# One ring of seven buffers for weight and conditioning tiles, and a conditioning rate of 0.6 in the state-space stage

## The chip, the cores and the metric

The kernel runs on one core of one Trainium2 chip. The metric is device time in microseconds (us); lower is better. Three runs of the kernel before gave a median of 2463.67 us (2461.16 to 2466.41).

## The reference, cut to what matters

A trunk of two layers in float32 on 256 tokens of 2048 channels. Each layer has a token mixer and a squared-ReLU MLP. Each of these four sub-layers sees a normalised input that is shifted and scaled, and its output is added through a gate. The shifts, scales and gates come from a conditioning vector `c`, through a matrix of 2048 x 12288 for each layer.

```python
cond = jax.nn.silu(c)
for i in range(DEPTH):                       # 2 layers
    mod = cond @ ada_w[i] + ada_b[i]         # (2048) x (2048, 12288)
    sh1, sc1, g1, sh2, sc2, g2 = jnp.split(mod, 6, axis=-1)
    h = modulate(rmsnorm(x, ln1_g[i]), sh1, sc1)
    y = stick_breaking_mixer(...) if i == 0 else s5_mixer(...)
    x = x + g1[:, None, :] * y
    h = modulate(rmsnorm(x, ln2_g[i]), sh2, sc2)
    x = x + g2[:, None, :] * sq_relu_mlp(h, mlp_w1[i], mlp_w2[i])
```

Mixer 0 is stick-breaking attention (`sb_w_in` 2048 x 6144, `sb_w_out` 2048 x 2048). Mixer 1 is a diagonal state-space layer, called S5 (`s5_w_in` 2048 x 2048), then a gated linear unit, GLU (`s5_w_glu` 2048 x 4096). Each MLP has two matrices of 2048 x 8192 and 8192 x 2048.

## The kernel before, in words

**Weight tiles.** Every large product is cut into tiles of 512 KB (1024 float32 in each of 128 partitions). `weights` (L126) loads one into a buffer `w`, with a DMA issued on SyncE's queue (L129). ScalarE rounds it to `wh` (L131) and VectorE forms the rest `wl = w - wh` (L133). TensorE then runs 24 matmuls of 256 or 258 columns (`cols_tile`, L160 to L162), or 12 of 512 (`gemm_rows`, L146 to L148). A buffer `w` is free again when L133 has read it. There are `nw` = 3 buffers `w`, and `nh` = 3 each of `wh` and `wl`, which become free when TensorE has read them.

**Ticks and stages.** After each weight tile `tick` (L101) runs: one tick for one weight tile, 736 in all. In this order: attention 128 ticks (96 of `sb_w_in`, 32 of `sb_w_out`), the MLP of layer 0 with 256, the S5 stage with 32 (`s5_w_in`, beside the state-space work), the GLU with 64, and the MLP of layer 1 with 256.

**Conditioning tiles.** `ada_load` (L262) loads 512 KB of `ada_w` into a buffer `adaw`, of which there are 4 (apart from a pool of 8 that only the first 16 tiles use). There are 384 such tiles, 32 for each of twelve vectors (shift, scale and gate of four sub-layers). From the first MLP on a tile is read by one VectorE instruction, which multiplies it by the conditioning vector and adds it to an accumulator `adsums` or `adacc` (L356; L354 for a first one). In the attention stage it takes two instructions of half the size (L368, L370), or, for some tiles, TensorE reads it (L296). A generator for each vector (`ada_dve`, `ada_pe`) yields after each tile. `pump` (L396), called in each tick, adds `rate` to a credit and takes one tile from the queue of generators for each whole credit. `drain` takes all that a stage still needs, at once. Two units after a vector's last tile TensorE sums its accumulators over the partitions (`totals`, L323), and the accumulators are free again; there are three of them from the first MLP on, each serving 16 tiles.

**Rates.** Attention runs at 0.85 and later 1.3. The MLP of layer 0 begins at 1.0, and at 0.42 from its 17th tick on (`between`). The S5 stage runs at 0.35, the GLU at the number of tiles left over 44 ticks (`pace(44, mid[-1])`, L1122), and the MLP of layer 1 at what is left over 140 ticks (L1253).

**Order.** TensorE and GpSimd keep the order in which the program is written. The instructions of SyncE, VectorE and ScalarE are ordered when the program is built: at each step the planner gives an engine the earliest instruction in the program whose operands and buffers are at hand by its reckoning. A load has no operand to wait for, only a buffer. That order is then fixed; on the chip each queue runs it one after the other.

Of the kernel before, what the change touches and what calls it, by code (L numbers as in the profile page):

```python
# [8 lines left out]
F32 = mybir.dt.float32  # L9
# [7 lines left out]
P = 128  # L17
# [39 lines left out]
class Trunk:  # L57
# [203 lines left out]

    def ada_load(self, layer, vec, g, t, wide=False):  # L262
        start = g == 0 and vec < 2 and layer == 0
        wt = (self.ap0 if start else self.wp).tile([P, 2, 512], F32, name="adaw", bufs=8 if start else 4)
        c0 = vec * D + g * 512
        w = self.i["ada_w"][layer]
        if wide:
            self.nc.sync.dma_start(wt, w[t * P:t * P + P, c0:c0 + 1024].rearrange("p (a b) -> p a b", a=2))
        else:
            self.nc.sync.dma_start(wt, w[2 * t * P:2 * t * P + 2 * P, c0:c0 + 512].rearrange("(a p) b -> p a b", p=P))  # L270
        return wt
# [910 lines left out]

    def run(self):
        nc = self.nc
        self.nw, self.nh = 3, 3
        self.rate, self.credit, self.pending = 0.0, 0.0, {}
        self.recorder, self.early = None, True
        self.left, self.acts, self.unit, self.sums, self.turn = {}, [], 0, None, 0
        self.now, self.plan = 0, {}
        self.ctx.enter_context(self.tc.manual_schedule(engines={mybir.EngineType.PE, mybir.EngineType.Pool}))  # L1190
        st = ExitStack()
        self.ap0 = st.enter_context(self.tc.tile_pool(name="ap0", bufs=6))
        self.logexp()
        self.consts()
        self.xT = self.pers.tile([P, NB, S], F32, name="xT")
        self.mod = [self.pers.tile([P, 96], F32, name="mod%d" % l) for l in range(2)]
        sets = [self.ada(0, [(1, g), (0, g)], on_pe=bool(5 >> g & 1)) for g in range(4)]
        gates = [self.ada(0, [(4, g), (3, g), (4, g + 1), (3, g + 1)], on_pe=bool(0 >> (g // 2) & 1)) for g in (0, 2)]
        self.queue += sets + [self.ada_vec(0, 2, on_pe=bool(0))] + gates
        with self.tc.tile_pool(name="tmp0", bufs=1) as self.sp_:  # L1200
            self.condition()
            for _ in range(4):
                self.step(sets[0])
            x = self.load_x()
            self.vectors()
            for _ in range(6):
                self.step(sets[0])
            self.flip_x(x)
            self.rms_rows()
        self.drain(sets[0])  # L1210
        st.close()
        self.open_h(self.pers)
        self.modulate(0, 4)
        self.attention(sets, gates[0])
        self.dump("x1")
        M = lambda i: bool(0 >> i & 1)
        self.sums = self.ctx.enter_context(self.tc.tile_pool(name="sums", bufs=1))
        mid = [self.ada_vec(1, 4, M(4)), self.ada_vec(1, 3, M(5))]
        nxt = [self.ada_vec(1, 1, M(1)), self.ada_vec(1, 0, M(2))]
        self.queue += [self.ada_vec(0, 5, M(0))] + nxt + [self.ada_vec(1, 2, M(3))] + mid  # L1220
        last = self.ada_vec(1, 5, M(6))
        self.dram = self.ctx.enter_context(self.tc.tile_pool(name="dram", bufs=1, space=bass.MemoryType.DRAM))
        self.rate = 1.0

        stp = ExitStack()

        def params():
            tmp = stp.enter_context(self.tc.tile_pool(name="s5t", bufs=1))
            self.s5_tables(tmp)

        def between():
            self.drain(gates[1])
            self.shifts(8, 16, 0, 1)
            for kb in range(8, 16):
                self.fold(kb, 0, 1)
            self.rate = 0.42
            params()

        def ready():
            self.recorder.play(None)  # L1240
            stp.close()
            self.drain(*nxt)
            self.open_h(self.pers)
            self.shifts(0, 16, 1, 0)

        self.mlp(0, nxt=ready, between=between)
        self.dump("x2")
        self.rate = 0.35
        self.s5_mixer(mid)
        self.dump("x3")  # L1250
        self.logexp()
        self.queue.append(last)
        self.pace(140, last)  # L1253
        self.rows_open()
        self.mlp(1, last=True)
# [28 lines left out]
```

## Time and profile before

| what | value |
|---|---|
| median of 3 runs | 2463.67 us (2461.16 to 2466.41) |
| profiled execution | 2467.97 us, its span 2466.1 us |
| TensorE (PE) busy | 2365.1 us, 96% of the span |
| VectorE (DVE) busy | 1795.4 us, 73% |
| ScalarE (ACT) busy | 1212.7 us, 49% |
| GpSimd (POOL) busy | 316.6 us, 13% |
| granted TensorE clock | 0.989 of full speed, mean |
| moved by DMA | 627.09 MB, 254 GB/s on average |

The page is of one execution. The stages need different things, so its averages say little of any of them; the rows further down cut the span into stages. Matmuls overlap one another, so a TensorE that shows busy all the time is not at its peak; a gap in it is time lost for certain. "DMA" in a row is the mean busy share of the core's 16 DMA engines.

### The profile page before, as it was taken

The numbers are of one execution on the slowest core, as the hardware profiler recorded it, in microseconds if no ns is written. First come the engines' busy times: TensorE is split into PE (matmuls) and PEld (weight loads), VectorE is DVE, ScalarE is ACT, GpSimd is POOL, SyncE is SP. The second block draws the span as 40 slices with busy tenths as digits, with TensorE's granted clock in tenths as the row PEclk, the third lists the DMA queues.
The fourth block names the chain that finished last, engine by engine and source line by source line (L and its number), as shares of the span: only waits on it lengthen the run. The fifth ranks groups of instructions, "written<-read, shape, count | busy, mean of one in ns | idle before, by whom it ended". The sixth has DMA issues, their size and how long they took to land.

```text
span 2466.1 us, 45235 instructions
## 1 busy us (share of the span) xinstructions
PE 2365.1 (96%) x18355; PEld 2160.4 (88%) x18355; DVE 1795.4 (73%) x2223; ACT 1212.7 (49%) x1814; POOL 316.6 (13%) x340
## 2 busy tenths in 40 slices
PE   7999999999998999889999999989999999999999
PEld 4777789899988899889998998989998998998987
DVE  5789999999778767875786668888744554555554
ACT  4534875346334335435546776434554543543543
POOL 0000110001056545445300000000000000000000
PEclk9999999999999999999999999999999999999999
DMA  9888899999999967997798544999856555556565
GB/s 341 302 299 306 288 308 320 322 303 294 310 310 315 300 207 230 309 299 219 259 316 276 174 154 159 314 329 314 281 175 192 184 186 190 175 179 193 180 195 164
DMA packets 416773, 627.09 MB, mean 254 GB/s; under 512 B 19858, under 2 KB 282420, under 8 KB 414260
## 3 DMA queue, kind: packets, MB, share of 16 engines
q1 hardware_dynamic: 411968, 606.16, 74.8%
q0 software_dynamic: 3968, 17.83, 2.2%
q8 instruction: 144, 2.36, 0.4%
q14 instruction: 65, 0.53, 0.1%
q10 hardware_dynamic: 628, 0.21, 0.0%
HBM read 607.34 MB, written 16.78 MB: 253 GB/s over the span
## 4 chain that ended last, share of the span: by engine, by line
PE 44%; DMA 6%; DVE 5%; issue 3%; ACT 0%; SPq 0%; DVEq 0%; ACTq 0%
PE acc L160 9%; PE acc L162 8%; PE acc L161 8%; DMA adaw<-in_ada_w 5%; PE acc L146 5%; PE acc L148 5%; PE acc L147 5%; DVE wl L133 2%; PE mp L1053 1%; DVE adsums L356 1%; PE mp L1078 1%; PE mp L1038 1%; PE mp L1015 1%; DVE xT L435 1%; DMA w<-in_s_w_glu 0%
## 5 line engine op out<-in xcount | busy, mean ns | idle before, releaser
L131 ACT ACTIVATE wh<-w 128x1024 fp32r<-128x1024 f32 x736 | 777.5, 1058 | 1030.9 <-PE acc L162 364.6
L133 DVE TENSOR_TENSOR wl<-w,wh 128x1024 fp32r<-128x1024 f32 x736 | 922.6, 1255 | 436.9 <-ACT wh L131 434.3
L160 PE MATMUL acc<-hH,wl 128*128 128x258 f32 (+1 forms) x2816 | 808.4, 287 | 28.4 <-DVE wl L133 26.1
L162 PE MATMUL acc<-hH,wh 128*128 128x258 f32 (+1 forms) x2816 | 799.2, 284 | 0.0
L161 PE MATMUL acc<-hL,wh 128*128 128x258 f32 (+1 forms) x2816 | 797.8, 283 | 0.2 <-DVE hL L123 0.2
L160 PEld LDWEIGHTS acc<-hH,wl 128*128 128x128 f32 x2816 | 535.8, 190 | 44.3 <-DVE wl L133 33.6
L161 PEld LDWEIGHTS acc<-hL,wh 128*128 128x128 f32 x2816 | 536.3, 190 | 0.6 <-DVE hL L123 0.4
L162 PEld LDWEIGHTS acc<-hH,wh 128*128 128x128 f32 x2816 | 534.8, 190 | 0.0
L160 PE MATMUL acc<-aH,wl 128*128 128x256 f32 x1024 | 294.3, 287 | 26.4 <-DVE wl L133 25.5
L161 PE MATMUL acc<-aL,wh 128*128 128x256 f32 x1024 | 289.5, 283 | 0.0
L162 PE MATMUL acc<-aH,wh 128*128 128x256 f32 x1024 | 289.4, 283 | 0.0
L356 DVE SCALAR_TENSOR_TENSOR adsums<-adaw,cond,adsums 128x1024 f32<-128x1024 f32 x150 | 199.1, 1328 | 53.6 <-DMA adaw<-in_ada_w 53.0
L160 PEld LDWEIGHTS acc<-aH,wl 128*128 128x128 f32 x1024 | 194.3, 190 | 34.1 <-DVE wl L133 33.7
L146 PE MATMUL acc<-wh,aL 128*128 128x512 f32 x512 | 202.2, 395 | 0.0
L148 PE MATMUL acc<-wh,aH 128*128 128x512 f32 x512 | 202.1, 395 | 0.0
L147 PE MATMUL acc<-wl,aH 128*128 128x512 f32 x512 | 202.0, 395 | 0.0
L161 PEld LDWEIGHTS acc<-aL,wh 128*128 128x128 f32 x1024 | 194.4, 190 | 0.0
L162 PEld LDWEIGHTS acc<-aH,wh 128*128 128x128 f32 x1024 | 194.2, 190 | 0.0
L370 DVE SCALAR_TENSOR_TENSOR adacc<-adaw,cond,adacc 128x512 f32<-128x512 f32 x240 | 179.2, 750 | 3.1 <-DMA adaw<-in_ada_w 1.3
L146 PE MATMUL acc<-wh,hL 128*128 128x512 f32 x384 | 157.5, 410 | 5.8 <-ACT wh L131 3.1
L147 PE MATMUL acc<-wl,hH 128*128 128x512 f32 x384 | 153.8, 401 | 3.3 <-DVE wl L133 3.2
L148 PE MATMUL acc<-wh,hH 128*128 128x512 f32 x384 | 152.9, 398 | 0.0
(311 smaller groups left out, 2751.0 us busy)
## 6 DMA issues: line engine op xcount, KB each, us to landing
w<-in_mlp_w SPq DMA_DIRECT2D x512, 512.0 KB, 4.0
adaw<-in_ada_w SPq DMA_DIRECT2D x384, 512.0 KB, 6.0
w<-in_sb_w_in SPq DMA_DIRECT2D x96, 512.0 KB, 5.2
w<-in_s_w_glu SPq DMA_DIRECT2D x64, 512.0 KB, 5.4
w<-in_sb_w_out SPq DMA_DIRECT2D x32, 512.0 KB, 5.7
w<-in_s_w_in SPq DMA_DIRECT2D x32, 512.0 KB, 4.8
pw<-W POOLq DMA_DIRECT2D x8, 1024.0 KB, 6.5
W<-pw SPq DMA_DIRECT2D x8, 1024.0 KB, 7.7
```

The source lines that it names most:

```text
L131: nc.scalar.activation(h, w, AF.Copy)
L133: nc.vector.tensor_tensor(l, w, h.bitcast(F32), op=OP.subtract)
L146: nc.tensor.matmul(o, aL(kb)[:, s], H[:, kk], start=(kb == k0), stop=False)
L147: nc.tensor.matmul(o, aH(kb)[:, s], L[:, kk], start=False, stop=False)
L148: nc.tensor.matmul(o, aH(kb)[:, s], H[:, kk], start=False, stop=(kb == k1 - 1))
L160: nc.tensor.matmul(o, L[:, kk, s], aH(kb), start=(kb == k0), stop=False)
L161: nc.tensor.matmul(o, H[:, kk, s], aL(kb), start=False, stop=False)
L162: nc.tensor.matmul(o, H[:, kk, s], aH(kb), start=False, stop=(kb == k1 - 1))
L356: nc.vector.scalar_tensor_tensor(acc, wt, c, acc, op0=OP.mult, op1=OP.add)
L370: nc.vector.scalar_tensor_tensor(acc, wt[:, kk], c, acc, op0=OP.mult, op1=OP.add)
L435: nc.vector.scalar_tensor_tensor(x, y, self.mod[layer][:, vec * 16 + kb:vec * 16 + kb + 1], x, op0=OP.mult, op1=OP.add)
L1015: nc.tensor.transpose(pe[:, q * P:q * P + P], E[:, c, q].rearrange("p j a e -> p (j a e)"), self.ident)
```

## The change

The buffers of the two kinds of tile become one set. `nw` goes from 3 to 7, and `ada_load` takes its tile under the name `w`, with the same count, instead of `adaw` with 4. Both tiles have 4 KB in each partition, so the memory is the same (3 + 4 = 7). The first 16 tiles keep their own pool. The rate in the S5 stage goes from 0.35 to 0.6.

```diff
     def ada_load(self, layer, vec, g, t, wide=False):
         start = g == 0 and vec < 2 and layer == 0
-        wt = (self.ap0 if start else self.wp).tile([P, 2, 512], F32, name="adaw", bufs=8 if start else 4)
+        wt = self.ap0.tile([P, 2, 512], F32, name="adaw", bufs=8) if start else self.wp.tile([P, 2, 512], F32, name="w", bufs=self.nw)
...
     def run(self):
         nc = self.nc
-        self.nw, self.nh = 3, 3
+        self.nw, self.nh = 7, 3
...
         self.mlp(0, nxt=ready, between=between)
         self.dump("x2")
-        self.rate = 0.35
+        self.rate = 0.6
         self.s5_mixer(mid)
```

## Rows read from the trace of the kernel before

**Rows 1.** The page's 40 equal slices of the span, 61.65 us each.

```profile
PE   7999999999998999889999999989999999999999
...
DVE  5789999999778767875786668888744554555554
...
DMA  9888899999999967997798544999856555556565
GB/s 341 302 299 306 288 308 320 322 303 294 310 310 315 300 207 230 309 299 219 259 316 276 174 154 159 314 329 314 281 175 192 184 186 190 175 179 193 180 195 164
```

**Rows 2.** Windows by stage: length, busy time of each engine, clock, DMA share, GB/s.

```profile
0.00:491.10 491.10, 462.51 (x2441) 366.48 (x2442) 422.13 (x717) 266.69 (x524) 24.27 (x41) 0.98 0.92 311
491.10:592.00 100.90, 98.70 (x784) 94.50 (x783) 95.37 (x169) 53.82 (x79) 4.79 (x6) 1.00 0.92 305
592.00:1303.40 711.40, 672.04 (x5482) 659.34 (x5481) 552.77 (x559) 311.57 (x386) 282.45 (x282) 0.99 0.85 279
1303.40:1476.30 172.90, 167.02 (x2565) 154.97 (x2564) 114.07 (x153) 121.09 (x244) 5.13 (x11) 0.99 0.61 199
1476.30:1716.40 240.10, 225.58 (x2394) 215.63 (x2392) 201.65 (x247) 112.95 (x176) 0.00 (x0) 0.99 0.81 277
1716.40:1815.70 99.30, 94.89 (x774) 94.69 (x775) 71.19 (x75) 52.94 (x74) 0.00 (x0) 0.97 0.78 255
```

**Rows 3.** The same windows, conditioning tiles (adaw) alone: PE, PEld and DVE work.

```profile
592.00:1303.40 711.40, 0.00 (x0) 0.00 (x0) 164.65 (x121) 0.99 0.85 279
1303.40:1476.30 172.90, 0.00 (x0) 0.00 (x0) 3.85 (x3) 0.99 0.61 199
1476.30:1716.40 240.10, 0.00 (x0) 0.00 (x0) 78.50 (x63) 0.99 0.81 277
1716.40:1815.70 99.30, 0.00 (x0) 0.00 (x0) 21.25 (x17) 0.97 0.78 255
```

**Rows 4.** Windows of 16 ticks each, columns as in Rows 2.

```profile
1007.20:1061.50 54.30, 48.93 (x396) 47.10 (x394) 47.28 (x45) 19.79 (x23) 30.63 (x28) 1.00 0.91 311
...
1157.30:1204.20 46.90, 46.90 (x394) 46.90 (x393) 30.64 (x31) 25.67 (x34) 21.43 (x22) 1.00 0.67 211
...
1557.90:1611.00 53.10, 49.72 (x411) 48.06 (x409) 44.55 (x56) 22.11 (x30) 0.00 (x0) 1.00 0.97 332
...
1906.10:1952.20 46.10, 46.10 (x361) 44.92 (x361) 23.79 (x23) 23.75 (x29) 0.00 (x0) 1.00 0.60 185
```

**Rows 5.** Two of those windows, conditioning tiles alone.

```profile
1007.20:1061.50 54.30, 0.00 (x0) 0.00 (x0) 18.90 (x13) 1.00 0.91 311
...
1557.90:1611.00 53.10, 0.00 (x0) 0.00 (x0) 20.05 (x17) 1.00 0.97 332
```

**Rows 6.** Waits of SyncE's queue, 592 to 907 us: total us, times, longest.

```profile
SPq L129 <- DVE wl L133: 212.6, 95, 5.8
```

**Rows 7.** Waits of the engines, 592 to 907 us.

```profile
ACT wh L131 <- DMA w<-in_mlp_w: 106.0, 48, 5.6
```

**Rows 8.** DMA issues, 592 to 907 us, last column: median us from issue to landing.

```profile
w<-in_mlp_w SPq DMA_DIRECT2D x97, 512.0 KB, 5.0
adaw<-in_ada_w SPq DMA_DIRECT2D x61, 512.0 KB, 6.2
```

**Rows 9.** Groups of instructions on the page: busy us, mean ns, idle before.

```profile
L131 ACT ACTIVATE wh<-w 128x1024 fp32r<-128x1024 f32 x736 | 777.5, 1058 | 1030.9 <-PE acc L162 364.6
L133 DVE TENSOR_TENSOR wl<-w,wh 128x1024 fp32r<-128x1024 f32 x736 | 922.6, 1255 | 436.9 <-ACT wh L131 434.3
...
L356 DVE SCALAR_TENSOR_TENSOR adsums<-adaw,cond,adsums 128x1024 f32<-128x1024 f32 x150 | 199.1, 1328 | 53.6 <-DMA adaw<-in_ada_w 53.0
```

**Rows 10.** Chain of waits, 1040 to 1090 us: start, us, what.

```profile
1057.27 0.37 SPq L129
1057.68 10.39 DMA adaw<-in_ada_w
```

**Rows 11.** Waits of SyncE's queue, 185 to 491 us.

```profile
SPq L270 <- DVE adacc L370: 68.8, 64, 4.8
```

## The prediction

> **What bounds the kernel now.** I read the page's slices first (counted from 0). TensorE reads 8 tenths in slices 12, 16, 17 and 26; there the DMA engines read 9, and so they do in all of slices 5 to 13. In slices 14, 18, 19 and 22 to 24 it is the other way round: TensorE reads 9, and the DMA engines 4 to 7, with 154 to 259 GB/s [rows 1]. So the kernel swings between stretches that wait for data and stretches in which the DMA engines have time to spare. The windows by stage give the sizes [rows 2]. The second window (attention's end is at 491 us) and the first are VectorE's as much as the DMA's: 95.4 of 100.9 us busy there. From 592 to 1303 us, 224 ticks of the first MLP take 711.4 us, 3.18 us a tick. The GLU takes 240.1 us for 64 ticks. The S5 stage, 1303 to 1476 us, moves 199 GB/s and has TensorE nearly full.
>
> The third view is conditioning work by stage [rows 3]: 121 instructions in the 224 MLP ticks, 3 in the S5 stage, 63 in the GLU, 17 in the next 99 us. By the rates it should be otherwise: 224 x 0.42 = 94, and 32 x 0.35 = 11 in the S5 stage. Conditioning runs ahead of its pace. The reason lies in the order that the planner makes: a weight load waits for one of three buffers, a conditioning load finds one of its own four free, and so it goes first, until the three accumulators are full and TensorE's `totals` must empty one. So conditioning comes in bursts: 13 tiles in one 16-tick window [rows 5], none in another; the first takes 54.3 us, the second 46.9 [rows 4].
>
> The fourth view is the waits. Between 592 and 907 us SyncE's queue stands 212.6 us, in 95 waits, for a weight buffer that VectorE has not yet released [rows 6], and ScalarE waits 106.0 us for weights still on their way [rows 7]. A weight tile holds its buffer for 5.0 us of transfer [rows 8] and at least 1.06 + 1.26 us of rounding and subtraction [rows 9], 7.3 us, and longer where a wait lies between. Three buffers then give a tile each 2.4 us at the very best; with 2 us of waiting, each 3.1. The chain shows a wait at its worst: a conditioning load issued 0.4 us after a weight load takes 10.39 us to land [rows 10], and VectorE, in its fixed order, holds the next subtraction behind it.
>
> **The change part by part.** *One ring.* Both loads now ask for the same seven buffers and neither has anything else to wait for. So the earliest in the program gets the next one, and the loads go out in program order: conditioning keeps its pace. No instruction is added or removed; 384 and 736 loads stay. What moves is when. In program order 154 conditioning tiles are out when the first MLP begins, 16 more by its 17th tick at 1.0 and 7 by its 33rd at 0.42, 177 in all (180 today, from 384 - 121 - 3 - 63 - 17). The next 224 ticks bring 94 (today 121). I take the terms stage by stage.
>
> *224 ticks of the MLP.* The floor is the window without conditioning: 46.9 us for 16 ticks, 2.93 us a tick, TensorE without a gap, GpSimd's table work beside it [rows 4]. Can the DMA engines keep up? A window with weights alone has a share of 0.60 over 46.1 us, so a weight tile takes 27.7 / 16 = 1.73 us of the 16 engines. With 17 conditioning tiles beside 16 weights, 0.97 x 53.1 = 51.5 us; less the weights, 23.8 / 17 = 1.40 us for one of them [rows 4, 5]. The tables' transfers: 0.67 x 46.9 - 27.7 = 3.7 us in 16 ticks, 0.23 a tick [rows 4]. Sum: 1.73 + 0.42 x 1.40 + 0.23 = 2.55 us in a tick of 2.93, 87%. VectorE: 552.8 us of work today [rows 2] less 27 x 1.33 us, in some 660 us. So TensorE bounds this stretch, and a ring that holds about five weights (7 / 1.42) ahead covers a landing of 6 us and even one of 10. The bounds: 224 x 2.93 = 656 us, a gain of 55; or, if 87% of the engines is already too close to their end, the 3.1 us that three buffers give today, 694 us, a gain of 17. I take 2.96 us, near the floor, since the only row of a stretch without a burst is the floor itself: 663 us, a gain of 48.
>
> *First 32 ticks of the MLP.* VectorE is busy 95.4 of 100.9 us [rows 2]; three conditioning tiles fewer are 4 us of its work. I take 3; bounds 0 and 6.
>
> *S5 stage, rate 0.6.* 32 x 0.6 = 19 tiles instead of 3 instructions. They are hidden: the DMA share is 0.61, and 16 x 1.40 us over 172.9 us adds 0.13; VectorE goes from 114.1 by 16 x 1.33 to 135 us of 172.9 [rows 2, 9]. Each instruction can stand ahead of a subtraction or of the state-space chain for 1.3 us; three `wh` and `wl` in hand cover that, and if that cover is gone it costs at most 16 x 1.33 = 21 us. I take a loss of 1.
>
> *GLU.* In program order 177 + 94 + 19 = 290 tiles are out at its start and 62 remain, at (62 + 1) / 44 = 1.43 a tick over 44 ticks (1.59 at the old rate). A tick needs 1.73 + 1.43 x 1.40 = 3.73 us of the DMA engines, at their share of 0.96 [rows 4] 3.89 us: this stretch stays bound by them. The last S5 work holds TensorE in the first 8 ticks: the first 16 took 1557.9 - 1476.3 = 81.6 us against 46.1 for plain ones [rows 4], of which I give 28 to S5 and 8 to data. So 8 x 2.88 + 28 = 51 us; 36 x 3.89 = 140 less the 11 us that seven loaded tiles are worth, 129; and 20 ticks with weights alone, 58. Sum 238 against 240.1 [rows 2], a gain of 2; bounds a loss of 8 (no use of the loaded tiles) and a gain of 12 (44 ticks at a share of 1).
>
> A page would have it shorter: the Trainium skill ("DMA: Bandwidth & Descriptors", section "Where 436 GB/s comes from") gives about 358 GB/s from HBM to one core, by which 2.43 tiles of 0.524 MB would take 3.56 us, an estimate that makes the GLU 12 us shorter. The trace does not reach that rate in any stage: 332 GB/s at a share of 0.97 is the most that these windows show [rows 4].
>
> *Second MLP.* The last 32 tiles go out over 140 ticks instead of in a burst: 1.73 + 0.236 x 1.40 = 2.06 us a tick, hidden under 2.88. The stretch from 1716 us takes 99.3 us for 32 ticks [rows 2], against 92 by the plain window; the start of the normalisation keeps some 3 of it. Gain 4; bounds 0 and 7. The rest of that MLP shows TensorE at 9 tenths in every slice [rows 1] and in its plain window without a gap [rows 4], so deeper prefetch is worth nothing there.
>
> *Attention.* The old order already keeps to the pace there (two accumulators allow no more), and VectorE's work, 422 us in 491 [rows 2], is the same. I take 0. Bounds: a gain of 12, if looser buffers fill half of the 29 us in which TensorE is idle there, and a loss of 15, which is the last rival's beginning.
>
> *Sum.* 48 + 3 - 1 + 2 + 4 + 0 = 56 us. The profiled execution took 2467.97 us, so 2412; it stands 4.3 us above the median of the runs shown, so that a median would be 2407.7. I predict 2408.
>
> **Rivals.** *The DMA engines bind in the MLP (14%).* For it: a share of 0.91 over the 54.3 us window in which TensorE is busy for 48.9 [rows 4]. Against it: the queue's waits there are for buffers, not for the engines [rows 6], and 2.55 us of 2.93 leaves room. Then 3.1 us a tick: the gain is 17 + 3 - 1 + 2 + 4 = 25, and the median 2439.
>
> *The order does not follow the program (7%).* Were conditioning loads still taken first, bursts would stay and the ring would only be wider: every stage as today, 2464. Against it: the burst today is explained by the weights' lack of a buffer alone.
>
> *A slower attention stage (10%).* The place: 64 waits, 68.8 us, in which SyncE's queue stands for a conditioning buffer while VectorE is behind [rows 11]. Weights with three buffers of their own are already loaded when that happens. In one ring a late conditioning tile takes a buffer from a weight, and TensorE stops. The price is up to one wait each, 68.8 / 64 = 1.1 us, for the 112 tiles of the queue-bound part (64 waits seen, at most all of them): 120 us. From 56 / 112 = 0.5 us a tile on, this eats the whole gain; at 0.7 the median is 2486. Against it: VectorE bounds that stage, so its total work sets the time in either order.
>
> **How the numbers follow.** My forecast has 65%, the three rivals 14, 7 and 10%, and 4% go to a better case (attention gains 12 and GLU 12: 2385). The range goes from 2378, the floor in the MLP (7 more) and the gains of attention, GLU and second MLP at their bounds, to 2446, the first rival with 7 us lost in the S5 stage. The forecast's own range is 2390 to 2425. A difference under 0.2%, 5 us, is what a measurement of this kernel can't tell from none. Faster: 65 + 14 + 4 = 83%; within 0.2%: the 7% of the second rival; slower: 10%.
>
> **What would show it.** Right: in the profile after, conditioning instructions in the 224 ticks near 94 and near 19 in the S5 stage, spread evenly; those ticks at 2.96 us; SyncE's queue waiting as long as before but ScalarE's waits for `in_mlp_w` mostly gone; the second MLP beginning without its burst of 17 conditioning instructions. The GLU would still show a DMA share of 0.95 in its first two thirds. Wrong: a first window longer than 500 us, conditioning still in bursts, or a TensorE with gaps in the MLP while the DMA share stands above 0.9.

## The result, and the profile after

The changed kernel takes 2520.35 us (median of 4 runs, 2515.32 to 2526.05) beside 2463.99 us for the kernel before (4 runs): a ratio of 1.023, 95% interval 1.0202 to 1.0258. It is slower by 56 us; I had forecast 56 us faster. The profiled span went from 2466.1 to 2515.1 us.

The page's slices, now 62.9 us each:

```profile
PE   7999999999898898888989999999999999999999
...
DVE  5699999998566776656766889896665566555554
...
DMA  9888899998777777777778766897667777655654
GB/s 350 288 309 301 283 313 317 342 324 266 228 233 256 245 247 228 224 249 241 251 224 282 252 213 217 272 363 234 210 217 235 230 226 230 196 181 187 183 194 131
```

From slice 10 to slice 20 every engine has time to spare: TensorE drops to 8 tenths, VectorE reads 5 to 7, the DMA engines 7. Nothing there is at its limit, unlike before [rows 1]. The windows by stage, cut at the same weight tiles as in [rows 2]:

```profile
0.00:488.40 488.40, 461.68 (x2447) 362.91 (x2447) 423.10 (x717) 265.90 (x524) 24.61 (x41) 0.99 0.92 313
488.40:584.80 96.40, 94.36 (x755) 91.27 (x756) 94.84 (x176) 53.97 (x79) 8.68 (x8) 1.00 0.97 318
584.80:1356.80 772.00, 690.77 (x5498) 676.00 (x5498) 510.17 (x526) 312.25 (x386) 265.97 (x281) 0.97 0.76 240
1356.80:1531.00 174.20, 169.88 (x2584) 158.04 (x2584) 136.20 (x171) 121.30 (x245) 5.14 (x11) 0.98 0.75 249
1531.00:1767.70 236.70, 221.88 (x2353) 212.89 (x2352) 192.78 (x241) 110.76 (x173) 0.00 (x0) 0.97 0.82 270
1767.70:1864.70 97.00, 95.97 (x803) 95.76 (x802) 60.98 (x65) 53.94 (x74) 0.00 (x0) 1.00 0.70 220
```

| stage | before, us | after, us | difference | forecast |
|---|---|---|---|---|
| attention | 491.1 | 488.4 | -2.7 | 0 |
| first MLP, 32 ticks | 100.9 | 96.4 | -4.5 | -3 |
| first MLP, 224 ticks | 711.4 | 772.0 | **+60.6** | -48 |
| S5 | 172.9 | 174.2 | +1.3 | +1 |
| GLU | 240.1 | 236.7 | -3.4 | -2 |
| second MLP, 32 ticks | 99.3 | 97.0 | -2.3 | -4 |

Five of six terms came out within 3 us. The whole error sits in one stage. There the engines' waits (us in total, times, longest), those of GpSimd left out, are:

```profile
ACT wh L131 <- PE acc L162: 361.9, 168, 7.6
DVE adsums L356 <- DMA w<-in_ada_w: 144.1, 52, 6.0
PEld acc L160 <- DVE wl L133: 94.7, 58, 4.3
DVE adacc L356 <- DMA w<-in_ada_w: 81.4, 28, 5.8
PE acc L160 <- DVE wl L133: 81.0, 54, 4.1
```

ScalarE no longer waits for weights, as it did in [rows 7]: they lie loaded in the ring. But VectorE now waits for conditioning loads. With L354's 12.7 us it is 238 us; before it was some 44 in this stage, nearly all of it in these two lines of the kernel before (592 to 1303.4 us):

```profile
DVE adsums L356 <- DMA adaw<-in_ada_w: 27.8, 23, 3.6
DVE adacc L356 <- DMA adaw<-in_ada_w: 15.7, 16, 2.9
```

VectorE's work and these waits are 510 + 238 = 748 of the 772 us: the engine that reads 66% busy sets the pace. And TensorE waits for `wl`, which VectorE forms. One place in VectorE's timeline (start, us, instruction, idle time before it) and in SyncE's queue shows how:

```profile
1007.28 1.22 DVE L133 TENSOR_TENSOR wl<-w,wh 128x1024 fp32r<-128x1024 f32 x1
1008.41 0.15 DVE L287 SCALAR_TENSOR_TENSOR mod<-mod,colv 128x4 f32<-128x4 f32 x1
1008.49 1.22 DVE L133 TENSOR_TENSOR wl<-w,wh 128x1024 fp32r<-128x1024 f32 x1
1013.87 1.28 DVE L356 SCALAR_TENSOR_TENSOR adsums<-w,cond,adsums 128x1024 f32<-128x1024 f32 x1 [4.17 <-DMA w<-in_ada_w]
1015.08 1.22 DVE L133 TENSOR_TENSOR wl<-w,wh 128x1024 fp32r<-128x1024 f32 x1
1016.21 0.68 DVE L497 TENSOR_TENSOR rl<-acc,rms 128x514 f32<-128x514 f32 x1
1016.81 1.21 DVE L133 TENSOR_TENSOR wl<-w,wh 128x1024 fp32r<-128x1024 f32 x1
```

```profile
1008.52 0.34 SPq L268 DMA_DIRECT2D w<-in_ada_w  x1
1009.73 6.96 SPq L129 DMA_DIRECT2D w<-in_mlp_w  x3
1018.05 0.34 SPq L268 DMA_DIRECT2D w<-in_ada_w  x1
```

The subtraction that ends at 1008.50 us frees a buffer; the conditioning load is issued at 1008.52 us. One more subtraction follows, until 1009.71 us, and next in VectorE's order is the instruction that reads this very tile: VectorE stands idle for 4.17 us, until the load has landed. The subtractions behind it, whose weights are there, stand with it.

### The profile page after: what moved, and what is told of

It reads as the page before. It is cut to its first block, busy times and chain, and to the rows that moved or that the text cites. A ratio compares the mean times of both kernels' runs of the same rounds, so it can differ in the third digit from the quotient of the medians.

```text
span 2515.1 us, 45267 instructions
## 1 busy us (share of the span) xinstructions
PE 2378.9 (95%) x18355; PEld 2171.8 (86%) x18355; DVE 1784.2 (71%) x2223; ACT 1211.8 (48%) x1814; POOL 304.4 (12%) x340
## 4 chain that ended last, share of the span: by engine, by line
PE 39%; DMA 6%; DVE 4%; issue 2%; ACT 0%; DVEq 0%; ACTq 0%
PE acc L160 7%; PE acc L162 7%; PE acc L161 7%; DMA w<-in_ada_w 5%; PE acc L147 5%; PE acc L148 5%; PE acc L146 5%; DVE wl L133 2%; PE mp L1053 1%; DMA w<-in_s_w_glu 1%; DVE adsums L356 1%; PE mp L1015 1%; PE mp L1038 1%; PE mp L1078 0%; DVE adacc L356 0%
## 5 line engine op out<-in xcount | busy, mean ns | idle before, releaser
L160 PE MATMUL acc<-hH,wl 128*128 128x258 f32 (+1 forms) x2816 | 814.7, 289 | 54.5 <-DVE wl L133 52.3
L162 PE MATMUL acc<-hH,wh 128*128 128x258 f32 (+1 forms) x2816 | 803.7, 285 | 0.0
L160 PEld LDWEIGHTS acc<-hH,wl 128*128 128x128 f32 x2816 | 540.8, 192 | 74.3 <-DVE wl L133 60.9
L162 PEld LDWEIGHTS acc<-hH,wh 128*128 128x128 f32 x2816 | 539.8, 192 | 0.0
L160 PE MATMUL acc<-aH,wl 128*128 128x256 f32 x1024 | 295.0, 288 | 38.5 <-DVE wl L133 38.4
L356 DVE SCALAR_TENSOR_TENSOR adsums<-w,cond,adsums 128x1024 f32<-128x1024 f32 x150 | 195.0, 1300 | 190.9 <-DMA w<-in_ada_w 190.7
L162 PE MATMUL acc<-aH,wh 128*128 128x256 f32 x1024 | 291.8, 285 | 0.0
L160 PEld LDWEIGHTS acc<-aH,wl 128*128 128x128 f32 x1024 | 196.5, 192 | 44.1 <-DVE wl L133 44.1
L162 PEld LDWEIGHTS acc<-aH,wh 128*128 128x128 f32 x1024 | 196.6, 192 | 0.0
L370 DVE SCALAR_TENSOR_TENSOR adacc<-w,cond,adacc 128x512 f32<-128x512 f32 x240 | 179.9, 752 | 4.1 <-DMA w<-in_ada_w 1.9
```

The costliest lines, as they stand in the source:

```text
L160: nc.tensor.matmul(o, L[:, kk, s], aH(kb), start=(kb == k0), stop=False)
L162: nc.tensor.matmul(o, H[:, kk, s], aH(kb), start=False, stop=(kb == k1 - 1))
L356: nc.vector.scalar_tensor_tensor(acc, wt, c, acc, op0=OP.mult, op1=OP.add)
L370: nc.vector.scalar_tensor_tensor(acc, wt[:, kk], c, acc, op0=OP.mult, op1=OP.add)
```

## Experiments

Theory A: the ring is full of waiting weights, so a conditioning load gets its buffer only when a subtraction frees one, and VectorE's fixed order has the instruction that reads it right behind; load time stands in series with VectorE's work. Counted in the trace of the changed kernel, in these 224 ticks: where a conditioning load has m weight loads ahead of it, its VectorE instruction has m - 5 subtractions ahead of it in 60 of 96 cases and m - 4 in 35. (The expectations below say five or six, one too many.) Of these 96 loads 80 were released by a subtraction. The rivals: B, the rate of 0.6; C, an even mix of loads is too much for the DMA engines; D and E below. Ratios are against the kernel before, measured again with each group of runs (medians of 2464.66 to 2466.17 us); the times of stages are of one profiled execution each.

**The ring alone**

```diff
-        self.rate = 0.6
+        self.rate = 0.35
```

> The shared ring of seven, the rate in the S5 stage back at 0.35. Theory A (VectorE stands at a conditioning instruction whose load was issued only just before it, because a full ring gives that load its buffer late): the loss of the change sits in the 224 ticks of the first MLP, which this kernel has unchanged, so about 2520 us (2512 to 2530). Theory B (the rate of 0.6 is what costs): back to about 2464 us or below. Theory C (weights and conditioning mixed evenly are too much for the DMA engines in the first MLP): also about 2520 us.

2531.45 us, ratio 1.0273 (1.0247 to 1.03), 1.5 us above the range of A and C. The 224 ticks take 776.0 us, the GLU 247.6 us instead of 236.7. The loss is the ring's; the rate takes some 11 us off it in the GLU. B falls.

**The rate alone**, in the kernel before:

```diff
-        self.rate = 0.35
+        self.rate = 0.6
```

> The two sets of buffers as before (3 and 4), the rate in the S5 stage 0.6. Theory A and C: buffers and accumulators, not the rate, set when conditioning runs there, so 2455 to 2468 us, within 10 us of before. Theory B: 2500 us or more.

2458.07 us, ratio 0.9971 (0.9958 to 0.9985): as A and C had it, a little faster. The S5 stage still holds 3 conditioning instructions, and the GLU goes from 240.1 to 235.9 us.

**The ring, and the instructions at their own place.** The edge (`NoSync` stands for a longer expression of the kernel) only orders VectorE's own instructions: each one of L354 and L356 behind the last subtraction that stands before it in the program. It moves the lines below by three or four, so that L163, L165, L357 and L359 in the rows that follow are the old L160, L162, L354 and L356.

```diff
-        nc.vector.tensor_tensor(l, w, h.bitcast(F32), op=OP.subtract)
+        self.cut = nc.vector.tensor_tensor(l, w, h.bitcast(F32), op=OP.subtract)
...
+    def behind(self, made):
+        self.tc.add_manual_dep(made.ins, self.cut.ins.name, NoSync, reason="pace")
...
-                        nc.vector.scalar_tensor_tensor(acc, wt, c, acc, op0=OP.mult, op1=OP.add)
+                        made = nc.vector.scalar_tensor_tensor(acc, wt, c, acc, op0=OP.mult, op1=OP.add)
+                    self.behind(made)
```

> The changed kernel, and each conditioning instruction of VectorE from the first MLP on is put behind the subtraction of the weight tile that stands before it in the program, instead of five or six subtractions earlier; loads, order of loads and work are the same. Theory A: the load then has five ticks (14 us) to land in, the stalls go, the 224 ticks take about 665 us instead of 772, in all 2410 us (2400 to 2430). Theory C (DMA engines): nothing changes in what they must move per tick, so 2510 to 2525 us.

2399.65 us, ratio 0.9731 (0.9708 to 0.9754), at the lower end of what A had. The windows of the 224 ticks and of the GLU, in this kernel:

```profile
589.70:1240.60 650.90, 650.90 (x5462) 647.96 (x5461) 524.09 (x520) 311.49 (x385) 297.19 (x274) 1.00 0.89 284
...
1409.30:1650.90 241.60, 225.20 (x2367) 215.36 (x2366) 199.75 (x246) 111.71 (x175) 0.00 (x0) 0.98 0.83 279
```

and its longest waits in those 224 ticks, in which VectorE's wait for conditioning loads is gone:

```profile
ACT wh L131 <- PE acc L165: 308.0, 179, 2.4
POOL t L962 <- ACT CT L958: 235.1, 8, 73.1
DVE wl L133 <- ACT wh L131: 99.7, 117, 2.1
```

The same loads, all 1120 tiles in the same order, with more bytes a second (284 GB/s at a share of 0.89) and no gap in TensorE: 121 us less in this stage than in the changed kernel. C falls; A's place and size hold. The 650.9 us are 12 below my forecast of 663 for this stage, and 5 below the floor of 656 that I had set.

**The placing without the ring.** The same edit in the kernel before, with its 3 + 4 buffers and 0.35.

> The kernel before (3 buffers for weights, 4 for conditioning, rate 0.35) with the same placing of the conditioning instructions behind their weight tile's subtraction: conditioning keeps its pace without a shared ring. Theory A, and the part of my prediction that bursts and three late weight buffers cost 3.18 us a tick: the 224 ticks take 670 to 690 us instead of 711, in all 2425 us (2410 to 2445), above the run with ring and placing by what deeper weight prefetch is worth. Theory C: no gain, 2460 us or more.

2423.97 us, ratio 0.9832 (0.9809 to 0.9856); 224 ticks and GLU:

```profile
590.60:1252.60 662.00, 656.69 (x5463) 649.69 (x5462) 517.99 (x521) 312.36 (x385) 283.03 (x274) 1.00 0.87 279
1421.70:1673.10 251.40, 226.45 (x2365) 215.30 (x2364) 208.25 (x253) 112.36 (x174) 0.00 (x0) 0.98 0.84 283
```

So 49 of the 60 us that the 224 ticks can lose come back by the placing alone, and TensorE has gaps of 5 us left. Conditioning keeps its pace: 6 to 8 instructions in each 16 ticks, 94 in all, instead of 0 to 16, 121 in all. Burstiness goes with the old kernel's loss, as I had it; but the placing also takes away VectorE's 44 us of waits for conditioning loads in this stage, and no run separates the two. The tiles that no longer run ahead come later: the GLU takes 251.4 us instead of 240.1, so that the whole kernel gains 41 us. The ring, once its own stall is gone, adds 11 us in the 224 ticks.

**How early is too early.** The edge goes to the subtraction of the weight tile four ticks earlier, and two; a list `cuts` keeps the subtractions. Against the edit above:

```diff
-        self.cut = nc.vector.tensor_tensor(l, w, h.bitcast(F32), op=OP.subtract)
+        self.cuts.append(nc.vector.tensor_tensor(l, w, h.bitcast(F32), op=OP.subtract))
...
-        self.tc.add_manual_dep(made.ins, self.cut.ins.name, NoSync, reason="pace")
+        self.tc.add_manual_dep(made.ins, self.cuts[-1 - 4].ins.name, NoSync, reason="pace")   # or -1 - 2
```

> The changed kernel; each conditioning instruction is put behind the subtraction of the weight tile four ticks before its own in the program: one or two places earlier than that the planner may not put it (in the changed kernel it stands five or six ticks ahead). So about one subtraction lies between the release that starts the load and the instruction that needs it. Theory A (load time in series with VectorE's work): a cycle for 2.38 ticks of 5.5 us landing, 1.3 us, and about 1.4 instead of 2.4 subtractions with what lies beside them, some 6.7 instead of 8.3 us; near TensorE's 6.9, so most of the loss comes back: 2405 to 2450 us. Theory D (it is not the landing; conditioning must simply stand at its own place in the program): no better than 2490 us.

2441.01 us, ratio 0.9894 (0.9878 to 0.9909). The stage and VectorE's longest waits for loads in it, with those of L357 132 us:

```profile
589.60:1282.40 692.80, 667.61 (x5487) 658.62 (x5486) 515.12 (x524) 311.30 (x386) 277.62 (x281) 0.99 0.85 268
```

```profile
DVE adsums L359 <- DMA w<-in_ada_w: 84.3, 42, 5.2
DVE adacc L359 <- DMA w<-in_ada_w: 40.1, 23, 4.8
```

> The same with two ticks: three or so subtractions, 8.7 us of ticks, lie between the load's start and the instruction. Theory A: longer than a landing of 5 to 6 us, so no stall is left: 2395 to 2410 us, as with the placing at its own tick (2400). Theory D: between 2400 and 2520 in proportion, some 2440 us.

2393.44 us, ratio 0.9703 (0.9688 to 0.9718), and

```profile
586.60:1239.50 652.90, 652.85 (x5474) 649.49 (x5473) 525.46 (x524) 312.20 (x386) 299.88 (x281) 1.00 0.89 283
```

```profile
DVE adsums L359 <- DMA w<-in_ada_w: 4.1, 3, 2.7
```

The order "where the planner puts it, four ticks early, two ticks early, at its tick" gives 772, 693, 653 and 651 us, and waits of 238, 132, 4 and 0 us. An order in which 60 of 96 instructions stand one subtraction later brings 79 us back. D falls: two ticks early is as good as none. The whole kernel is even 1.6 us below what I had expected of A; its GLU takes 234.0 us, 7.6 less than with each instruction at its own tick.

**A shorter ring**, five buffers in the changed kernel:

```diff
-        self.nw, self.nh = 7, 3
+        self.nw, self.nh = 5, 3
```

> The changed kernel with five buffers in the ring instead of seven. Theory A: what counts is that the ring is full of waiting weights when a conditioning tile asks, not how many they are; the instruction is still planned right behind its load, so 2515 to 2550 us. Theory E (the deep ring itself delays things, by transfers in the wrong order or too many at a time): a shorter ring is better, 2500 us or less.

2601.88 us, ratio 1.0552 (1.0526 to 1.0578), 52 us above the range that I expected of theory A, and above that of E.

```profile
0.00:530.80 530.80, 477.85 (x2446) 371.59 (x2447) 426.83 (x717) 265.62 (x523) 24.09 (x41) 0.96 0.86 286
630.80:1424.50 793.70, 695.57 (x5476) 678.34 (x5476) 510.63 (x525) 311.59 (x388) 260.30 (x281) 0.96 0.74 233
```

The 224 ticks take 793.7 us, 22 more than with seven, and VectorE's waits for conditioning loads in them are 256 us, so E falls. What I had left out is the attention stage, 42 us longer: there a tick brings 1.2 conditioning tiles, and ScalarE's waits for weights rise from 57 to 117 us. That five buffers for both kinds are too few there fits this, but no run shows it; nor is it shown why the 224 ticks lose 22 us more.

**A higher rate in the S5 stage**, ring and instructions at their tick:

```diff
-        self.rate = 0.6
+        self.rate = 0.9
```

> Ring of seven with the conditioning instructions at their own ticks, and a rate of 0.9 in the S5 stage: 10 tiles more go there, 10 fewer into the GLU's first 44 ticks, which the DMA engines bound at 1.40 us for each tile. If S5 hides them as it hid the first 18: 14 us less in the GLU, 2386 us (2380 to 2394). If VectorE (1.3 us each, in a stage where it is busy four fifths) holds the state-space chain: 2397 to 2405 us.

2387.36 us, ratio 0.968 (0.9663 to 0.9697). S5 and GLU:

```profile
1237.60:1408.00 170.40, 169.81 (x2606) 157.36 (x2605) 143.20 (x182) 122.34 (x246) 5.13 (x11) 1.00 0.82 271
1408.00:1637.20 229.20, 219.98 (x2351) 211.26 (x2351) 187.14 (x232) 111.05 (x173) 0.00 (x0) 0.99 0.82 271
```

Ten more tiles cost the S5 stage 1.7 us and spare the GLU 12.4, 1.24 us a tile.

**The best version**: two ticks early, 0.9. Beside it, on the same chip, the changed kernel again.

> Ring of seven, conditioning instructions two ticks before their own, rate 0.9 in the S5 stage. Two ticks earlier shortened the first part of the GLU by 7.5 us against the placing at the own tick, 0.9 shortened the GLU by 12.4; both act on the DMA-bound ticks of the GLU. If they add: 2381 us (2376 to 2386). If the early placing only spares what 0.9 spares too: 2386 to 2390 us.

2382.6 us, ratio 0.9671 (0.9654 to 0.9687), 82 us faster than the kernel before; the two gains nearly add (6 and 12 us below the run with ring and placing, and 17 together).

> The changed kernel once more on the chip of the run beside it, so that the version with placing can be set against it: 2510 to 2530 us, with the wait of VectorE for conditioning loads in the 224 ticks of the first MLP within 20 us of the 238 us of its first profile.

2519.49 us, ratio 1.0225 (1.0204 to 1.0247); the 224 ticks take 772.3 us, and VectorE's waits there 241 us.

## Why the prediction was wrong, point by point

**What bounds the kernel: held.** Bursts of conditioning, taken first because weights lacked a buffer, went with the cost of the 224 ticks: with pace and no ring they take 662 us instead of 711. How much of the 49 us is the bursts' own, and how much VectorE's 44 us of waiting for loads, is open.

**Loads in program order: held.** 94 tiles were forecast for this stage, and 90 instructions of L356 and 6 of L354 ran in it; the S5 stage has 23 and 1, 24 in all (I had 19: they run four or five ticks early). They come evenly, 6 to 8 in each 16 ticks. Weights do lie ready in the ring.

**"So TensorE bounds this stretch, and a ring that holds about five weights (7 / 1.42) ahead covers a landing of 6 us and even one of 10": the step that failed.** It is true of the weights and false of the conditioning tiles. The term of 224 ticks counted VectorE by its busy time alone (some 517 in 660 us, measured 510) and put its waiting at nothing; it waited 238 us, and a gain of 48 us became a loss of 60.6. I followed the loads through the shared ring and did not ask the same of their readers. A weight that is loaded early is also read late: its subtraction waits for `wh`, thus for TensorE. A conditioning instruction waits for nothing but its tile, and in the planned order it stands early, four or five subtractions before its place. In the full ring its buffer becomes free hardly earlier than that: one or two subtractions end between the issue of the load and the reader, for 95 of the 96 instructions. So too little time was left between them for a landing of 4.9 us (the median of these loads in this stage), and what was missing stood in VectorE's line: 85 waits, 238 / 96 = 2.5 us for each tile, 60.6 + 60.5 = 121 us of time lost against the placed version. I had even shown this line of events in [rows 10], and 53 us of such waits in [rows 9], and took it for a burst's doing.

The Trainium skill says it shortly ("Perfetto Trace Analysis", section "Tensor Engine Instruction (MATMUL, LD_WEIGHTS)"): ScalarE, VectorE and GpSimd are "strict FIFO". The trace agrees: subtractions whose weights had landed long before stand 4.17 us behind one instruction that waits.

**DMA engines at 87%: held**, measured 0.89 in the placed version with TensorE full, so the first rival is out. **The second rival** (the order would not follow the program) was put for the loads, which do follow it; it is VectorE's order that does not, and I had asked nothing of it. **The third** (a slower attention stage) did not come: 488.4 us. It came near, with a late conditioning tile in front of weights, but in another stage and in another way: there the tile was to take a weight's buffer, while here the weights lay loaded and lacked VectorE's turn. In attention VectorE is busy for 423 of 488 us and waited 1.9 us before L370 for such loads; that the one is the reason of the other is not shown. **"What would show it"** named TensorE's gaps beside a DMA share above 0.9; the gaps came beside 0.76. Its signs of the loads' order all came, in a kernel that was slower: they told nothing of the readers.

**GLU, S5, second MLP**: right in sign and within 3 us. The GLU's sum had three parts: 51 us for 8 ticks, 129 for 36 ticks that the DMA engines bind, 58 for 20 with weights alone. The windows of these ticks in the changed kernel:

```profile
1531.00:1584.30 53.30, 50.56 (x888) 46.03 (x887) 49.54 (x75) 33.50 (x73) 0.00 (x0) 0.94 0.66 201
1584.30:1711.20 126.90, 114.82 (x996) 111.34 (x995) 112.65 (x129) 51.99 (x68) 0.00 (x0) 0.97 0.97 330
1711.20:1767.70 56.50, 56.50 (x474) 55.52 (x474) 30.59 (x39) 25.27 (x32) 0.00 (x0) 1.00 0.65 202
```

Each part came within 3 us, with a DMA share of 0.97 in the second. The 1.24 us a tile, from the run at 0.9, stand beside the 1.40 of my sum.

**The range**: its lower end is 2 us off its own terms; 7 + 12 + 10 + 3 us below 2408 are 2376, not 2378.

Why the planner places the instruction so early is open: its reckoning of a load's landing stands in no trace. That its order is the cause is shown, since moving these instructions, with all loads in the same order, takes the loss away.

## What to carry to other kernels

When two kinds of tile share buffers, ask of each kind how long before its reader the buffer comes free, not only how many buffers there are: a ring that is full of one kind gives the other its buffer at the last moment. Look at the reader's place in the order of its engine too; an engine that is 66% busy can still set the time if it waits in line, and busy plus waiting time shows that (748 of 772 us). One ordering edge, which held the reader back to within two subtractions of its own place, was worth 119 us in this stage; the pooled buffers, once it was there, 11.

## What the runs showed of the hardware that I had not expected

In the changed kernel one slice of 62.9 us, in the GLU, moved 363 GB/s, with both kinds of load in flight; my prediction had found no more than 332 in its windows. The Trainium skill ("DMA: Bandwidth & Descriptors", section "Where 436 GB/s comes from") gives about 358 GB/s from HBM as the limit of a core; the measurement is above it.

TensorE's granted clock stood lower where TensorE had gaps: 0.97 in the 224 ticks of the changed kernel, with 81 us of gaps, and 1.00 with the instructions placed, without a gap. The 0.97 is a mean of stretches at full and at half speed; 0.03 x 772 = 23 us, an estimate, is what the clock took of the 121 us that this stage lost against the placed version.
